# Storing the first image pair by halves and loading less ahead, in a sparse 3x3 convolution

## The chip, the cores and the metric

One core of one Trainium2 chip. The metric is device microseconds of a whole execution; "span" is the part of it that the profile covers, about 1.8 us shorter. Some executions of any kernel are slow as a whole (over 1.5% above the fastest of the same kernel); they are called slow below and are left out of every ratio.

## The reference, cut to what matters

```python
# x: 16 x 64 x 64 x 64 fp32, weight: 128 x 64 x 3 x 3 fp32 with 90% zeros
x_pad = np.pad(x, ((0, 0), (0, 0), (1, 1), (1, 1)))
for b, co, ci, kh, kw in ...:                      # five loops, written out in the original
    output[b, co] += weight[co, ci, kh, kw] * x_pad[b, ci, kh:kh+64, kw:kw+64]
```

An ordinary 3x3 convolution. The input is 16.8 MB, the output 33.6 MB, both fp32 in HBM.

## The kernel before

Two images make a pair: 64 input channels of each fill the 128 partitions. A pair has 4 blocks of 16 rows; I number the blocks of all pairs through as steps, step = 4 x pair + block. For each step but the first, POOL adds neighbouring rows (`s`), PE multiplies, ACT copies one shared product, DVE adds it to the others and writes fp32 rows of `o`, which SP stores. x is loaded by POOL's DMA queue, which casts fp32 to bf16 on the way.

```python
xs = [x_pool.tile([128, H, W], BF16, name=f"x{p}") for p in range(NP)]   # all of x stays on chip
nc.sync.dma_start(out=w_sb, in_=...)                                     # weights, fp32
nc.sync.dma_start(out=x_head[:, 0:HEAD, :], in_=pair(0)[:, 0:HEAD, :])   # "the head": 32 rows, fp32
nc.gpsimd.dma_start(out=xs[0][:, HEAD:H, :], in_=pair(0)[:, HEAD:H, :])
...
EARLY, CUT = 4, 24
for p in range(1, EARLY):
    load(p)                          # whole pairs up front
load(EARLY, 0, CUT)                  # and 24 rows of the next
...
keep_busy(27)                        # matmuls on zeros, to wake PE's clock
...                                  # weights are cast and transposed
keep_busy(28)
...
for p in range(NP):
    ...
    last = p == NP - 1
    for blk in range(4):
        ...
            twos(p, o, r0)
            if p == 1 and blk == 3:
                load(EARLY, CUT, H)
            elif p > 1 and blk == 3 and p + EARLY - 1 < NP:
                load(p + EARLY - 1)
        ...
        if last and blk % 2 == 1:    # last pair: stored by halves
            ...
    if not last:                     # others: stored whole, after the fourth block
        for n in range(2):
            nc.sync.dma_start(out=out[2 * p + n], in_=o[n])
```

Of the kernel before, what the change touches and what calls it, by code (L numbers as in the profile page):

```python
# [8 lines left out]
FP32 = mybir.dt.float32  # L9
BF16 = mybir.dt.bfloat16  # L10
# [17 lines left out]
def kernel(  # L28
# [6 lines left out]
    nc = tc.nc  # L35

    B, C_IN, H, W = x.shape
    C_OUT, _, KH, KW = weight.shape
    assert (B, C_IN, H, W) == (16, 64, 64, 64) and (C_OUT, KH, KW) == (128, 3, 3)
    NP = B // 2  # L40
    HEAD = 32

    const_pool = ctx.enter_context(tc.tile_pool(name="const", bufs=1))
# [4 lines left out]
    psum_pool = ctx.enter_context(  # L48
        tc.tile_pool(name="psum", bufs=8, space=bass.MemoryType.PSUM)
    )  # L50
# [4 lines left out]
    def pair(p):  # L55
        return x[2 * p : 2 * p + 2].rearrange("n i h w -> (n i) h w")
# [10 lines left out]
    def load(p, a=0, b=H):  # L67
        nc.gpsimd.dma_start(out=xs[p][:, a:b, :], in_=pair(p)[:, a:b, :])  # L68



    EARLY, CUT = 4, 24
    for p in range(1, EARLY):
        load(p)
    load(EARLY, 0, CUT)


    idle_rhs = const_pool.tile([128, 128], BF16, name="idle_rhs")
    nc.vector.memset(idle_rhs, 0.0)  # L79
    idle_ps = psum_pool.tile([128, 128], FP32, name="ps")  # L80

    def keep_busy(n):
        for _ in range(n):
            nc.tensor.matmul(idle_ps, idle_rhs, idle_rhs, start=True, stop=True)  # L84

    keep_busy(27)



# [8 lines left out]
    def cast_x(copy, a, b):  # L98
        copy(out=xs[0][:, a:b, :], in_=x_head[:, a:b, :])  # L99
# [24 lines left out]
    nc.vector.tensor_copy(out=wT[:, G0], in_=ps0)  # L124
    ps2 = transposed(G2)
    nc.scalar.copy(out=wT[:, G2], in_=ps2)
    keep_busy(28)
    cast_x(nc.scalar.copy, 9, 18)
    difference(G01, ps0)
    difference(G21, ps2)  # L130
# [26 lines left out]
    def direct(p, o, r0, rows):  # L157
        ps = product(
            [(xs[p], G1, r0, 1), (xs[p], G0, r0 - 1, 1), (xs[p], G2, r0 + 1, 1)], rows
        )  # L160
        nc.scalar.copy(out=o[0][:, r0 : r0 + rows, :], in_=ps[0])  # L161
        nc.vector.tensor_copy(out=o[1][:, r0 : r0 + rows, :], in_=ps[1])  # L162

    def twos(p, o, r0):
        t0 = r0 // 2
        s = s_pool.tile([128, 8, W], BF16, name="s")
        nc.gpsimd.tensor_tensor(  # L167
            out=s, in0=xs[p][:, r0 : r0 + 16 : 2, :], in1=xs[p][:, r0 + 1 : r0 + 16 : 2, :], op=ADD
        )
        shared = product([(s, G1, 0, 1)], 8)  # L170
        pc = []
        for n in range(2):
            c = p_pool.tile([128, 8, W], FP32, name="pc")
            nc.scalar.copy(out=c, in_=shared[n])  # L174
            pc.append(c)
        even = [(xs[p], G21, r0 + 1, 2), (xs[p], G0, r0 - 1, 2)]
        odd = [(xs[p], G01, r0, 2), (xs[p], G2, r0 + 2, 2)]
        for first, terms in ((r0, even), (r0 + 1, odd)):
            ps = product(terms, 8)
            for n in range(2):  # L180
                nc.vector.tensor_tensor(  # L181
                    out=o[n][:, first : r0 + 16 : 2, :], in0=ps[n], in1=pc[n], op=ADD
                )

    for p in range(NP):
        o = [o_pool.tile([C_OUT, H, W], FP32, name="o") for _ in range(2)]
        last = p == NP - 1
        for blk in range(4):
            r0 = 16 * blk
            if BLOCKS[p][blk] == "T":  # L190
                twos(p, o, r0)


                if p == 1 and blk == 3:
                    load(EARLY, CUT, H)
                elif p > 1 and blk == 3 and p + EARLY - 1 < NP:
                    load(p + EARLY - 1)
            else:
                for r, rows in ((r0, 8), (r0 + 8, 8)):
                    direct(p, o, r, rows)  # L200
            if last and blk % 2 == 1:
                for n in range(2):
                    rows = slice(r0 - 16, r0 + 16)
                    nc.sync.dma_start(out=out[2 * p + n][:, rows, :], in_=o[n][:, rows, :])
        if not last:
            for n in range(2):
                nc.sync.dma_start(out=out[2 * p + n], in_=o[n])

# [29 lines left out]
```

## Time and profile before

| | before |
|---|---|
| time, median of 4 runs beside the changed kernel | 126.5 us (126.4 to 126.55) |
| span of the profiled run | 124.7 us |
| first convolution matmul | 7.35 us |
| loads queued up front | 9.47 MB of HBM reads |
| first store issued | 21.83 us |
| HBM traffic | 50.62 MB |

The lines that carry this stand in the prediction below. To read them: a slice is 1/40 of the span, "DMA" is the share of time in which the 16 DMA engines have a packet open, and "GB/s" counts a casting load by the bf16 bytes that it writes, which is half of what it reads. So where I compare DMA work I use the load queue (q0) twice and the store queue (q1) once.

### The profile page before, as it was taken

The page shows a single profiled execution, that of the slowest core. Times are in us where ns is not written, and L with a number is a line of the kernel's source. Part 1 is how long each engine was busy: PE and PEld are TensorE (multiplying, and loading weights), DVE is VectorE, ACT ScalarE, POOL GpSimd, SP SyncE. Part 2 cuts the span into 40 slices and gives each one's busy share as a digit, 9 for nine tenths or more (in the row PEclk, how much of TensorE's full clock was granted, in tenths as well). Part 3 has the DMA queues.
Part 4 walks back from the last instruction along what each step waited for, and adds up shares of the span by engine and source line. Part 5 has one row for each costly group of instructions (what it writes and reads, how often), then busy time and mean ns, then how long its engine had stood idle before and what let it go on. Part 6 is the DMA issues. An engine that isn't in the chain of part 4 may idle for free.

```text
span 124.7 us, 2543 instructions
## 1 busy us (share of the span) xinstructions
PE 109.0 (87%) x1030; PEld 59.5 (48%) x1030; DVE 82.3 (66%) x135; ACT 39.0 (31%) x71; POOL 41.1 (33%) x46
## 2 busy tenths in 40 slices
PE   6999999999999999999999999999999999940000
PEld 6755555555555555555555555555555555510000
DVE  0354777877787778777877787778777878870000
ACT  4545323333333333333333333333333333300000
POOL 6427343533353335333533333333333300000000
PEclk9999999999999999999999999999999999998555
DMA  4999999999999999999999999999999999999991
GB/s 127 356 225 213 215 218 213 211 400 311 350 409 410 318 297 344 436 310 323 302 433 310 318 315 423 420 449 420 426 431 420 436 426 441 415 412 420 428 381 53
DMA packets 4188, 42.93 MB, mean 344 GB/s; under 512 B 464, under 2 KB 464, under 8 KB 976
## 3 DMA queue, kind: packets, MB, share of 16 engines
q1 hardware_dynamic: 2880, 34.90, 66.6%
q0 software_dynamic: 1296, 7.86, 30.8%
q8 instruction: 8, 0.13, 0.4%
q14 instruction: 4, 0.03, 0.1%
HBM read 17.07 MB, written 33.55 MB: 406 GB/s over the span
## 4 chain that ended last, share of the span: by engine, by line
PE 82%; DMA 5%; DVE 1%; issue 1%; DVEq 0%; SPq 0%
PE ps L148 82%; DMA o<-in_x_dram 5%; DVE o L181 1%; DVEq L233 0%; DVE x L99 0%; SPq L60 0%; DVEq L181 0%
## 5 line engine op out<-in xcount | busy, mean ns | idle before, releaser
L181 DVE TENSOR_TENSOR o<-ps,pc 128x512 f32<-128x512 f32 x124 | 77.8, 686 | 22.1 <-PE ps L148 19.8
L148 PE MATMUL ps<-x,wT 64*128 64x504 bf16 (+3 forms) x780 | 88.7, 373 | 0.3 <-DVE x L99 0.3
L148 PEld LDWEIGHTS <-wT 64*128 64x128 bf16 x966 | 54.4, 94 | 48.9 <-issue 0.3
L167 POOL TENSOR_TENSOR s<-x 128x512 bf16<-128x512 bf16 x31 | 35.6, 1151 | 57.5 <-PE ps L148 43.2
L174 ACT COPY pc<-ps 128x512 f32<-128x512 f32 x62 | 33.3, 589 | 64.0 <-issue 61.8
L148 PE MATMUL ps<-s,wT 64*128 64x512 bf16 (+1 forms) x186 | 25.7, 377 | 0.0
L84 PE MATMUL ps<-idle_rhs 128*128 128x128 bf16 x55 | 4.8, 265 | 1.0 <-DVE idle_rhs L79 1.0
L84 PEld LDWEIGHTS <-idle_rhs 128*128 128x128 bf16 x55 | 4.4, 123 | 1.0 <-DVE idle_rhs L79 1.0
L68 POOL DMA_DIRECT2D x<-in_x_dram x8 | 4.4, 561 | 0.0
L103 DVE CAST w_bf<-w_sb 128x192 bf16<-128x192 f32 (+1 forms) x4 | 1.1, 346 | 2.9 <-DMA w_sb<-in_weight_dram 2.9
L162 DVE COPY o<-ps 128x512 f32<-128x512 f32 x2 | 1.4, 692 | 2.0 <-PE ps L148 2.0
L161 ACT COPY o<-ps 128x512 f32<-128x512 f32 x2 | 1.2, 586 | 2.4 <-PE ps L148 2.4
L99 ACT CAST x<-o 128x576 bf16<-128x576 f32 (+1 forms) x2 | 1.5, 804 | 0.8 <-DMA o<-in_x_dram 0.8
L99 DVE CAST x<-o 128x576 bf16<-128x576 f32 x1 | 0.5, 460 | 1.9 <-DMA o<-in_x_dram 1.9
L103 ACT ACT_TABLE_LOAD x1 | 1.3, 1283 | 0.7 <-PEq L222 0.7
L109 PE MATMUL ps<-ident,w_bf 128*128 128x128 bf16 x9 | 1.1, 296 | 0.3 <-DVE w_bf L103 0.3
L103 ACT CAST w_bf<-w_sb 128x64 bf16<-128x64 f32 (+1 forms) x2 | 0.7, 416 | 1.8 <-DMA w_sb<-in_weight_dram 1.8
L109 PEld LDWEIGHTS <-w_bf 128*128 128x128 bf16 x9 | 0.8, 128 | 0.7 <-DVE w_bf L103 0.7
L113 DVE TENSOR_TENSOR wT<-ps,wT 128x384 bf16<-128x384 f32 x2 | 1.0, 548 | 0.0
L63 POOL DMA_DIRECT2D x<-in_x_dram x1 | 0.7, 693 | 0.8 <-POOLq L222 0.8
L79 DVE MEMSET idle_rhs<- 128x64 uint32 x1 | 0.1, 112 | 0.8 <-PEq L222 0.8
L122 ACT CAST wT<-ps 128x384 bf16<-128x384 f32 x1 | 0.5, 480 | 0.4 <-PE ps L109 0.4
(8 smaller groups left out, 2.0 us busy)
## 6 DMA issues: line engine op xcount, KB each, us to landing
out_dram<-o SPq DMA_DIRECT2D x14, 2048.0 KB, 17.4
x<-in_x_dram POOLq DMA_DIRECT2D x6, 1024.0 KB, 15.8
out_dram<-o SPq DMA_DIRECT2D x4, 1024.0 KB, 11.4
o<-in_x_dram SPq DMA_DIRECT2D x1, 1024.0 KB, 5.6
x<-in_x_dram POOLq DMA_DIRECT2D x1, 640.0 KB, 14.0
x<-in_x_dram POOLq DMA_DIRECT2D x1, 512.0 KB, 7.5
x<-in_x_dram POOLq DMA_DIRECT2D x1, 384.0 KB, 24.6
w_sb<-in_weight_dram SPq DMA_DIRECT2D x1, 288.0 KB, 3.0
```

The lines of the kernel that those rows point to most:

```text
L68: nc.gpsimd.dma_start(out=xs[p][:, a:b, :], in_=pair(p)[:, a:b, :])
L84: nc.tensor.matmul(idle_ps, idle_rhs, idle_rhs, start=True, stop=True)
L99: copy(out=xs[0][:, a:b, :], in_=x_head[:, a:b, :])
L103: copy(out=w_bf4[:, g, a:b, :], in_=w_v[:, k : k + b - a, :])
L109: nc.tensor.matmul(wps[:, j, :], src, ident, start=True, stop=True)
L113: nc.vector.tensor_tensor(out=wT[:, g], in0=wps, in1=wT[:, G1], op=SUB)
L148: nc.tensor.matmul(ps[n][:, lo:hi, c_lo:c_hi], tap(g, kw, n), src[q, a:b:step, c_lo + kw - 1 : c_hi + kw - 1], start=(i == 0), stop=(i == ...
L161: nc.scalar.copy(out=o[0][:, r0 : r0 + rows, :], in_=ps[0])
L162: nc.vector.tensor_copy(out=o[1][:, r0 : r0 + rows, :], in_=ps[1])
L167: nc.gpsimd.tensor_tensor(out=s, in0=xs[p][:, r0 : r0 + 16 : 2, :], in1=xs[p][:, r0 + 1 : r0 + 16 : 2, :], op=ADD)
L174: nc.scalar.copy(out=c, in_=shared[n])
L181: nc.vector.tensor_tensor(out=o[n][:, first : r0 + 16 : 2, :], in0=ps[n], in1=pc[n], op=ADD)
```

## The change

Its intent is to let the first stores start at 16 us and not at 22, by putting fewer loads ahead of them, and to make up for that with loads issued later. The 55 narrow matmuls on zeros become 14 wide ones.

```diff
-    EARLY, CUT = 4, 24
+    EARLY, CUT = 2, 56
     for p in range(1, EARLY):
         load(p)
     load(EARLY, 0, CUT)
+    later = {5: [(2, CUT), (3,)], 7: [(4,)], 11: [(5,)], 15: [(6,)], 19: [(7,)]}
-    idle_rhs = const_pool.tile([128, 128], BF16, name="idle_rhs")
+    idle_rhs = const_pool.tile([128, 512], BF16, name="idle_rhs")
 ...
-            nc.tensor.matmul(idle_ps, idle_rhs, idle_rhs, start=True, stop=True)
-    keep_busy(27)
+            nc.tensor.matmul(idle_ps, idle_rhs[:, 0:128], idle_rhs, start=True, stop=True)
+    keep_busy(7)
 ...
-    keep_busy(28)
+    keep_busy(7)
 ...
+    HALVES = (0, NP - 1)
 ...
-                if p == 1 and blk == 3:
-                    load(EARLY, CUT, H)
-                elif p > 1 and blk == 3 and p + EARLY - 1 < NP:
-                    load(p + EARLY - 1)
+                for args in later.get(4 * p + blk, ()):
+                    load(*args)
 ...
-            if last and blk % 2 == 1:
+            if p in HALVES and blk % 2 == 1:
 ...
-        if not last:
+        if p not in HALVES:
```

I call the loads issued after step 5 (8 rows of pair 2, then pair 3) "the reload".

More of the change, by code (lines that the diff above doesn't have):

```diff
@@ L75 @@
     load(EARLY, 0, CUT)
-    idle_rhs = const_pool.tile([128, 128], BF16, name="idle_rhs")
+    later = {5: [(2, CUT), (3,)], 7: [(4,)], 11: [(5,)], 15: [(6,)], 19: [(7,)]}
+    idle_rhs = const_pool.tile([128, 512], BF16, name="idle_rhs")
     nc.vector.memset(idle_rhs, 0.0)
-    idle_ps = psum_pool.tile([128, 128], FP32, name="ps")
+    idle_ps = psum_pool.tile([128, 512], FP32, name="ps")
     def keep_busy(n):
         for _ in range(n):
-            nc.tensor.matmul(idle_ps, idle_rhs, idle_rhs, start=True, stop=True)
-    keep_busy(27)
+            nc.tensor.matmul(idle_ps, idle_rhs[:, 0:128], idle_rhs, start=True, stop=True)
+    keep_busy(7)
     w_v = w_sb.rearrange("o (i k) -> o k i", k=KH * KW)
@@ L183, in twos @@
                 )
+    HALVES = (0, NP - 1)
     for p in range(NP):
         o = [o_pool.tile([C_OUT, H, W], FP32, name="o") for _ in range(2)]
-        last = p == NP - 1
         for blk in range(4):
```

## The prediction

> **What bounds the kernel now.** I read the page's head and its slices first, to see which resource never rests.
>
> ```profile
> span 124.7 us, 2543 instructions
> PE 109.0 (87%) x1030; PEld 59.5 (48%) x1030; DVE 82.3 (66%) x135; ACT 39.0 (31%) x71; POOL 41.1 (33%) x46
> ...
> DMA  4999999999999999999999999999999999999991
> GB/s 127 356 225 213 215 218 213 211 400 311 350 409 410 318 297 344 436 310 323 302 433 310 318 315 423 420 449 420 426 431 420 436 426 441 415 412 420 428 381 53
> DMA packets 4188, 42.93 MB, mean 344 GB/s; under 512 B 464, under 2 KB 464, under 8 KB 976
> ...
> q1 hardware_dynamic: 2880, 34.90, 66.6%
> q0 software_dynamic: 1296, 7.86, 30.8%
> ...
> HBM read 17.07 MB, written 33.55 MB: 406 GB/s over the span
> ```
>
> Each slice is 3.12 us. The DMA row is full from the second slice to the last but one, while PE has gone idle four slices before the end. The GB/s row seems to say that the first half runs at half rate. It does not: the loads cast fp32 to bf16 and are counted by what they write (42.93 MB moved, against 17.07 + 33.55 = 50.62 MB at HBM; the gap of 7.69 MB is about the 7.86 MB of the load queue q0). So 213 GB/s of pure loading is 426 GB/s read, the rate of pure storing.
>
> The bound on time is therefore 50.62 MB / 0.427 MB per us = 118.5 us, 0.427 being my middle of the store-only rows below. Then I asked by windows where the other 6 us of the span lie.
>
> ```profile
> 2.00:4.00 2.00, 2.00 (x20) 1.79 (x17) 0.20 (x1) 0.22 (x2) 1.93 (x5) 1.00 1.01 339
> ...
> 22.00:24.00 2.00, 2.00 (x24) 1.05 (x20) 1.40 (x3) 0.76 (x2) 1.46 (x2) 1.00 0.99 172
> 24.00:26.00 2.00, 2.00 (x22) 1.07 (x20) 1.45 (x3) 1.07 (x2) 1.05 (x1) 1.00 1.10 334
> ...
> 90.00:100.00 10.00, 10.00 (x98) 5.30 (x96) 7.76 (x13) 3.22 (x6) 3.58 (x4) 1.00 1.02 433
> 100.00:110.00 10.00, 10.00 (x96) 5.23 (x94) 7.82 (x13) 3.22 (x6) 0.00 (x0) 1.00 0.99 423
> ...
> 121.00:122.00 1.00, 0.00 (x0) 0.00 (x0) 0.00 (x0) 0.00 (x0) 0.00 (x0) 0.50 0.58 246
> 122.00:123.00 1.00, 0.00 (x0) 0.00 (x0) 0.00 (x0) 0.00 (x0) 0.00 (x0) 0.50 0.20 82
> 123.00:124.00 1.00, 0.00 (x0) 0.00 (x0) 0.00 (x0) 0.00 (x0) 0.00 (x0) 0.50 0.00 0
> ```
>
> The last three columns are granted clock, DMA share, GB/s. Lost are 1.8 us ahead of the first packet, about 2.8 us after 121 in which engines finish unevenly and the program closes, a dip at 22 to 24 where loads hand over to stores (172 where 213 is usual: 2 us x 41/213 = 0.4 us), and the rest in a slow first few us. There is no idle stretch of DMA to recover in the middle.
>
> The second candidate is PE. The chain of waits names it, and needs care.
>
> ```profile
> PE 82%; DMA 5%; DVE 1%; issue 1%; DVEq 0%; SPq 0%
> ...
> 7.35 102.09 PE ps L148 x954
> ```
>
> PE runs without a gap from 7.35 to 109.44, and the last DVE addition ends at 111.98. But that chain ends there, and the span goes on for 12.7 us of storing. The last two half stores, 2.10 MB, need 2.10 / 0.427 = 4.9 us plus about 2 us to land: a store queue with no backlog would have been done near 119. Hence the end is set by DMA with some 5 us of backlog in front of it, and PE has that slack at the end only.
>
> **What the Trainium skill says.** "DMA: Bandwidth & Descriptors", section "Where 436 GB/s comes from": the fabric ceiling is 435.2 GB/s for a core. The trace agrees: 423 to 433 in store-only windows, so at most 2 or 3% is left in the rate. The same page, "Issuing engines are not separate DMA queues": transfers started by different engines share the same 16 DMA engines and interleave. So a store started earlier takes its bandwidth from a load; the mixed slices agree (310 to 320 GB/s counted, where loads count half). The same page, "Anatomy of one DMA — SWDGE (gpsimd) path": about 2.0 us fixed plus bytes / 436 GB/s, mostly the receipt at the end. The trace's 288 KB weight load, though on the other path, lands in 3.0 us against an estimate of 2.7 from that. "TensorE: Matmul & The Clock Gate", section "Wait — 56ns, not 53.3ns?": 106.7 and 426.7 ns for 128 and 512 columns cold, 55.6 and 215.7 warm. The trace has 27 narrow ones in 3.06 us (113 each) and 28 in 1.73 us (62 each).
>
> **The change, part by part.**
>
> (a) Zeros on PE. 55 x 128 = 7,040 columns become 14 x 512 = 7,168. First batch: 7 x 427 = 2.99 us for 3.06; second: 7 x 216 = 1.51 for 1.73 (estimates from the page named). The memset is four times as wide, perhaps 0.2 us later. The first convolution matmul waits for the cast of the input head, which waits for its load (landing at 6.8), so 7.35 stays. 41 matmuls and weight loads vanish, worth nothing on the path.
>
> (b) Loads up front. A pair is 2.10 MB read. Before: weights 0.29 + four pairs 8.39 + 24/64 of one 0.79 = 9.47 MB, drained at 1.8 + 9.47/0.427 = 24.0 us, where the windows show stores taking over. After: 0.29 + 2 x 2.10 + 56/64 x 2.10 = 6.32 MB, drained at 16.6, or near 17.3 with the slow start.
>
> (c) Stores of pair 0.
>
> ```profile
> 13.37 2.51 DVE L181 TENSOR_TENSOR o<-ps,pc 128x512 f32<-128x512 f32 x4 [1.30 <-PE ps L148]
> ...
> 15.70 1.16 POOL L167 TENSOR_TENSOR s<-x 128x512 bf16<-128x512 bf16 x1
> ...
> 21.83 14.22 SPq L207 DMA_DIRECT2D out_dram<-o  x4
> ```
>
> Block 1 is done for image 0 one addition before 15.88, so its half can be issued near 15.3 and that of image 1 near 16.0, instead of both at 21.8. The second halves go out at the old time. They reach DMA just as the loads run dry at about 17.
>
> (d) Loads moved. The rest of pair 2 and pair 3 follow the sum of step 5, which ends at 16.86: issued at 16.9 and 17.4. The remaining pairs keep their places, after steps 7 (22.9), 11, 15 and 19. By 23 us both programs have asked for the same bytes: pairs up to 4 and the stores of pair 0, 0.29 + 10.49 + 4.19 = 14.97 MB, good until 1.8 + 14.97/0.427 = 36.9 us. The next stores are issued at 34.57 in the trace, about 2 us before that. From there on the two programs are the same.
>
> Sum on the path: bytes 0; rate about +0.1 (pair 0 goes in 8 KB rows); the old dip of 0.4 us is replaced by one at about 17, of the same kind but closer to empty, 0.3 to 1.0 us, and perhaps a smaller one where loads come back near 21. Net: 0 to +0.7 us; I take +0.2, and so 126.7 us.
>
> **The rivals.**
>
> Earlier stores bring the end forward. The intent of the change, and true if DMA had idle time in the first 22 us or if the last stores were late for want of an earlier start. The full DMA row speaks against both: each store byte moved to 17 displaces a load byte to later, one for one. The most it could give is the dip (0.4) and a luckier tail: 125.7.
>
> DMA starves near 17. Stores are released by DVE, loads by POOL, both behind PE. Should the first half come out 1 us later, or a fresh queue need 2 to 3 us to get under way (at 22 the first stores seem to flow only after 24), DMA lies partly idle between 17 and 19, and nothing makes that up, as the rest is full: 127.5 to 128.5. For it: only 1.3 to 2 us between issue and dry queue. Against: SP is waiting for DVE alone, so it issues at once.
>
> ```profile
> SPq L207 <- DVE o L181: 90.1, 14, 20.1
> ```
>
> Pair 3 comes late and stalls PE. Issued at 17.4, it shares DMA with the stores: 2.36 MB at half of 427 is 11 us, plus start and receipt, so it lands at 29 to 33. POOL first needs it at its step 12, which starts at 37.76 in the trace. A margin of about 5 us or more; and a stall of 1 or 2 us of PE would only eat slack at the end. I give it little.
>
> PE stays cold. If 7 wide matmuls fail to wake the clock, the first 16 convolution matmuls or so cost twice, about 1.7 us, and the first half is late by that: this feeds the second rival. The work per us is as dense as before, so unlikely.
>
> **Range and chances.** Mechanism: one resource, never idle, the same bytes in another order. So 126.7 us, with 125.7 to 127.8 for 8 in 10: down by the dip and the tail, up by a starved 1 us and a second dip. The 2% limits are 124.0 and 129.0. Faster needs 2.5 us, more than all the recoverable loss in the middle: 3%. Slower needs both starving and a cold clock: 4%. Within 2%: 93%.
>
> **What would show it.** Right: a DMA row full from slice 2 on; GB/s rising over 300 near 17 instead of 24, and the pure-store stretch at over 420 starting at the same 78 us as before; PE still gapless from about 7.35, its last matmul near 109.4; stores landing until about 123. Step (c): SP's first store issue near 15.3. Step (d): POOL's two loads at about 17. Wrong: a DMA share well under 1 near 17 to 19 or 36 (starving), PE waiting on anything after 7.4 (late load), or store windows above 435 GB/s, or a last packet ahead of 121 us, which would mean that the order of reads and writes does change the rate, which I say it does not.

## The result, and the profile after

The changed kernel took 128.3 us in the median of 4 runs (127.78 to 128.81), the kernel before 126.5 us. The ratio is 1.0143, 95% interval 1.0101 to 1.0184. Ratios here are the mean time of one kernel's fast runs over that of the other's of the same rounds, so not quite the ratio of the medians. It is slower by 1.4%, within the 2% that counts as the same, but outside the range that I gave, and its own runs lie a whole microsecond apart.

The head of the page of the changed kernel, as shown of before:

```profile
span 126.0 us, 2467 instructions
...
PE   6989999999999999999999999999999999930000
...
DMA  4999998999999999999999999999999999999991
GB/s 146 339 225 211 215 300 193 265 278 289 273 322 416 325 309 333 424 296 320 343 424 307 302 333 442 416 439 416 432 421 437 442 421 416 426 426 419 429 395 55
...
HBM read 17.07 MB, written 33.55 MB: 402 GB/s over the span
```

The bytes are the same, 402 GB/s stands where 406 stood, and the DMA row is as good as full again. But look at the GB/s row: the stores do come in at the sixth slice (300, near 16 to 19 us), and the seventh (19 to 22 us) falls to 193. The windows say more exactly where; the last three columns are granted clock, DMA share and GB/s:

```profile
16.00:18.00 2.00, 2.00 (x22) 1.07 (x20) 1.27 (x4) 1.06 (x2) 1.87 (x3) 1.00 0.96 270
18.00:20.00 2.00, 2.00 (x22) 1.08 (x20) 1.87 (x4) 0.73 (x2) 0.95 (x2) 1.00 0.95 364
20.00:22.00 2.00, 2.00 (x24) 1.06 (x21) 1.41 (x3) 0.35 (x1) 0.53 (x1) 1.00 0.87 120
22.00:24.00 2.00, 2.00 (x22) 1.11 (x20) 1.40 (x3) 1.08 (x2) 1.47 (x2) 1.00 1.02 269
```

From 20 to 22 us DMA counts as 87% busy and moves 120 GB/s. Even if all of it were loads counted at half, that would be 240 of the usual 427. A busy share says that packets were open, not that they moved. The queues' own rows tell the bytes (queue, packets, MB, share of the 16 engines' time). The changed kernel from 20 to 23 us:

```profile
q0 software_dynamic: 149, 0.25, 69.9%
q1 hardware_dynamic: 38, 0.24, 19.4%
```

and the kernel before at its own handover, 22 to 25 us:

```profile
q0 software_dynamic: 156, 0.47, 92.1%
q1 hardware_dynamic: 9, 0.15, 11.7%
```

Three microseconds at 427 GB/s are 1.28 MB at HBM. The changed kernel moved 0.24 + 2 x 0.25 = 0.74 MB and lost 1.3 us there; the kernel before moved 0.15 + 2 x 0.47 = 1.09 MB and lost 0.4 us. The difference, about 0.8 us, is most of the 1.3 us between the two spans. About 0.5 us more went just before, where the loads hand over to the stores, from 16 to 20 us:

```profile
q1 hardware_dynamic: 131, 1.02, 64.2%
q0 software_dynamic: 55, 0.24, 29.7%
```

That is 1.02 + 2 x 0.24 = 1.50 of 1.71 MB. The kernel before moved 2 x 1.28 MB from 16 to 22 us and lost nothing there.

Was there nothing to do? The timeline of the changed kernel says there was:

```profile
14.12 2.51 DVE L183 TENSOR_TENSOR o<-ps,pc 128x512 f32<-128x512 f32 x4 [1.30 <-PE ps L150]
...
16.12 7.32 SPq L206 DMA_DIRECT2D out_dram<-o  x4
...
17.22 1.10 POOL L68 DMA_DIRECT2D x<-in_x_dram  x2
```

The first half store was issued at 16.12 and the second one could be when DVE's fourth addition had ended, at 16.63 (SP waits for DVE alone); the reload was issued at 17.22 and about 17.8. The instruction that issues the second half store is long in this run:

```profile
16.65 2.30 SPq L206 DMA_DIRECT2D out_dram<-o  x1
```

In the kernel before, the 14 instructions of this kind took 0.35 us in the median and 1.35 us at most. Those requests are 2.10 + 2.36 MB, over 10 us of DMA work, all issued by 19.0 us. Yet in DMA's records the reload's first packet, of its 8-row piece, starts at 19.84, and the second image's half only at 20.98, when the first image's half is all but through. So DMA was not short of requests at 20 us. What it had open then was mostly the 8-row piece, in packets of 1 KB; the second half store and the large piece of the reload were issued but still to come.

The start was late too. The chain of waits of the changed kernel:

```profile
1.18 6.38 DMA o<-in_x_dram
...
8.09 102.09 PE ps L150 x954
```

In this run the head of the input landed at 7.55 us and not at 6.81, so PE began 0.74 us later, and the first stores with it. PE then ran as before, 102.09 us without a gap. This delay is not a second sum to add: the bytes that DMA failed to move account for the longer span by themselves (see the sum over all profiles).

### The profile page after: what moved, and what is told of

Read it like the earlier page. It is cut to its first block, busy times and chain, and to the rows that moved or that the text cites. A ratio compares the mean times of both kernels' runs of the same rounds, so it can differ in the third digit from the quotient of the medians.

```text
span 126.0 us, 2467 instructions
## 1 busy us (share of the span) xinstructions
PE 109.6 (87%) x989; PEld 57.5 (46%) x989; DVE 82.4 (65%) x135; ACT 39.0 (31%) x71; POOL 41.1 (33%) x46
## 4 chain that ended last, share of the span: by engine, by line
PE 81%; DMA 5%; DVE 1%; issue 1%; DVEq 0%; SPq 0%
PE ps L150 81%; DMA o<-in_x_dram 5%; DVE o L183 1%; DVEq L235 0%; DVE x L101 0%; SPq L60 0%; DVEq L183 0%
## 5 line engine op out<-in xcount | busy, mean ns | idle before, releaser
L183 DVE TENSOR_TENSOR o<-ps,pc 128x512 f32<-128x512 f32 x124 | 77.8, 685 | 22.1 <-PE ps L150 19.8
L86 PE MATMUL ps<-idle_rhs 128*128 128x512 bf16 x14 | 5.6, 568 | 1.2 <-DVE idle_rhs L81 1.2
L86 PEld LDWEIGHTS <-idle_rhs 128*128 128x128 bf16 x14 | 1.8, 137 | 3.7 <-issue 2.4
## 6 DMA issues: line engine op xcount, KB each, us to landing
out_dram<-o SPq DMA_DIRECT2D x12, 2048.0 KB, 17.8
```

The costliest lines, as they stand in the source:

```text
L86: nc.tensor.matmul(idle_ps, idle_rhs[:, 0:128], idle_rhs, start=True, stop=True)
L183: nc.vector.tensor_tensor(out=o[n][:, first : r0 + 16 : 2, :], in0=ps[n], in1=pc[n], op=ADD)
```

## The experiments

Fifteen runs, each on one chip beside its own runs of the kernel before. Of those, one (201.5 us) and two (131.36 and 128.66) were slow and are left out. Times of single runs are given where they differ; the profile shows one run of each.

I call "the hole" the stretch after the up-front loads in which DMA moves little. Theory: the time lost is DMA's, between 16 and 24 us, and it comes from the margin between the up-front loads running dry and the stores and reload reaching the engines. Rivals: the wide zeros delay the start; half stores or small pieces cost rate by themselves.

### Each part alone

**wide_only**: the kernel before with only the zeros changed.

```diff
-    EARLY, CUT = 2, 56
+    EARLY, CUT = 4, 24
-    later = {5: [(2, CUT), (3,)], 7: [(4,)], ...
+    later = {7: [(4, CUT)], ...
-    HALVES = (0, NP - 1)
+    HALVES = (NP - 1,)
```

(The diffs of this group are against the changed kernel.)

> The kernel before with the 14 wide zero matmuls alone; loads and stores as before. Hole theory (the loss is DMA left short of work at 20 to 22 us): 126.3 to 126.7 us, as before, and DMA full throughout. Rival, late start (the 0.74 us by which the first convolution matmul came later is due to the wide zeros and carries to the end): first convolution matmul near 8.1 us instead of 7.35 and 127.0 to 127.4 us.

Measured: 126.43 us beside 126.64, ratio 1.0005 (0.9962 to 1.0048). The late start was there: the second batch of zeros,

```profile
5.25 2.62 PE L86 MATMUL ps<-idle_rhs 128*128 128x512 bf16 x7
```

took longer than the 1.73 us of the narrow one, with 374 ns for each matmul, between the 427 and 216 ns of the prediction's estimate, and the first convolution matmul came at 7.79 us. With four pairs of loads queued this cost nothing: the hole theory holds here, and the rival falls for the loads of before.

**halves_only**: the loads and zeros of before, the first pair by halves.

```diff
-    EARLY, CUT = 2, 56      (and later, and the zeros)
+    EARLY, CUT = 4, 24      (as in the kernel before)
```

> The kernel before with the stores of the first pair in halves alone; loads as before, narrow zeros. Hole theory: loads still queue until 24 us, so nothing runs dry: 126.2 to 126.8 us, with stores mixed in from about 17 us. Rival (8 KB rows or the earlier mixing of stores with loads cost rate by themselves): 127.2 us or more with DMA full and a lower GB/s count in 16 to 24 us.

Measured: 126.85 us beside 126.64, just over the range that the theory gave, ratio 1.0024 (0.9998 to 1.0050). No dry spell (from 17 to 20 us it moved 0.14 + 2 x 0.49 = 1.12 of 1.28 MB), and no gain either, which fits the prediction's argument that a store moved forward displaces a load one for one.

**loads_only**: the shorter up-front loading and the reload, the first pair stored whole.

```diff
-    HALVES = (0, NP - 1)
+    HALVES = (NP - 1,)      (and the narrow zeros)
```

> The kernel before with the shorter up-front loading and the later reloading alone; the first pair stored whole at 22 us, narrow zeros. Hole theory: after the up-front loads end near 17.3 us there is nothing until the reloads' first packets near 20 to 21.7 us: about 3 us of DMA lost, 128.5 to 130 us, worse than the changed kernel. Rival (loads in smaller pieces are harmless, it is the half stores that hurt): 126.3 to 127 us.

Measured: 129.00 us, ratio 1.0172 (1.0136 to 1.0209; one of its four runs was slow at 130.53 and is left out). As the theory said. The half stores are the cure for the shorter loading, and an incomplete one.

**all_but_wide**: the changed kernel with narrow zeros.

```diff
-    idle_rhs = const_pool.tile([128, 512], BF16, ...      keep_busy(7) ... keep_busy(7)
+    idle_rhs = const_pool.tile([128, 128], BF16, ...      keep_busy(27) ... keep_busy(28)
```

> The changed kernel with the narrow zeros of before. Hole theory: the same as the changed kernel, 127.8 to 128.6 us, with the hole at 20 to 22 us. Rival, late start by wide zeros: first convolution matmul back at 7.35 us and 127.0 to 127.5 us.

Measured: 127.18 us (127.11 to 127.24, and one run of 128.47), ratio 1.0078 (1.0020 to 1.0136). Three of the four runs fell in the rival's range and one in the theory's, and the first convolution matmul was back at 7.35 us in the profiled run. That spoke for the rival; with two kinds of runs it did not decide about the zeros, and narrow_again below took it up.

### Moving the reload, the pieces and the zeros

**changed_again**: the changed kernel, unedited.

> The changed kernel once more, on the chip of the next three. Hole theory plus a late start by the wide zeros: 1.2 to 1.9 us over the kernel before of the same rounds; second batch of zeros 2.4 to 2.6 us long, first convolution matmul at 7.8 us or later, DMA short of work for about 2 us between 20 and 23 us. Rival (the kernel without the wide zeros differed from this one by chip or chance): 0.7 to 1.0 us over before.

Measured: 126.93, 126.97, 128.36 and 128.82 us; ratio 1.0095 (1.0012 to 1.0179). By the ratio that is 1.2 us over the kernel before, the low end of the theory's range, but in two kinds of runs of one kernel on one chip. The profile fell on a good run (126.97), with PE starting at 7.27 us and the second batch of zeros only 1.67 us long, which is not what I had expected.

**reload_at_3**: the reload two steps earlier.

```diff
-    later = {5: [(2, CUT), (3,)], 7: ...
+    later = {3: [(2, CUT), (3,)], 7: ...
```

> The changed kernel with the first reload (8 rows of pair 2, and pair 3) issued after the sum of step 3, near 12.5 us, not after that of step 5, near 17 us. Hole theory: the loads reach DMA before the first ones have drained, nothing runs dry, and the time is within 0.4 us of the kernel before, like the half stores alone. Rival (not the moment of the reload but the small pieces and 8 KB rows cost): no better than the changed kernel of this call.

Measured: 126.64 us beside 126.53, ratio 1.0019 (0.9978 to 1.0061). This one edit takes the loss away, with half stores, 8 KB rows, small pieces and wide zeros all kept. (Its interval and that of changed_again overlap; the pair with the late start below, reload_at_3_late and changed_late, is clearly apart.) It does not beat the kernel before either; none of the fifteen does. Its queues from 12 to 32 us (each GB/s figure is 0.5 us):

```profile
GB/s 180 182 201 229 201 215 215 215 248 201 29 121 320 178 182 410 147 442 131 410 180 360 262 262 311 213 344 426 410 426 442 344 246 279 295 213 295 295 213 377
...
q0 software_dynamic: 549, 2.92, 73.6%
q1 hardware_dynamic: 320, 2.37, 28.8%
```

There is still a dip at 17 to 18 us (29, 121). It is not a handover between the queues, as no store packet starts before 19.4 us: it lies between the last of the up-front loads and the first packets of the 8-row piece. From 19.5 us the two queues take turns every half microsecond (410 and 442 are stores, 147 and 131 loads counted at half).

**one_piece**: no 8-row piece.

```diff
-    EARLY, CUT = 2, 56
+    EARLY, CUT = 2, 64
-    later = {5: [(2, CUT), (3,)], 7: ...
+    later = {5: [(3,)], 7: ...
```

> The changed kernel with 64 rows of pair 2 up front instead of 56, so no 8-row piece: pair 3 is issued 0.55 us earlier and the up-front loads last 0.6 us longer. Hole theory: the hole shrinks by about 1 us, and the time comes to 0.4 to 1.0 us over before. Rival (the lost time is the handing over from stores back to loads, which takes its 1 to 2 us whenever it falls): the same as the changed kernel within 0.3 us.

Measured: 126.51, 126.53, 127.23 and 127.58 us; ratio 1.0032 (0.9980 to 1.0083). In the direction of the theory and about of its size, but the intervals of this kernel and the changed one overlap.

**wide_fewer**: 4 wide zeros in the second batch.

```diff
-    keep_busy(7)
+    keep_busy(4)
```

> The changed kernel with 4 instead of 7 wide zero matmuls in the second batch. If the wide zeros delay the first convolution matmul, and this delay widens the hole: the batch ends before 7 us, the first convolution matmul is back near 7.35 us when the input's head lands by 6.8, and the time is 0.6 to 1.0 us over before. Rival (the zeros are beside the point): the same as the changed kernel of this call within 0.2 us.

Measured: 126.84, 126.89, 127.75 and 127.84 us; ratio 1.0050 (0.9993 to 1.0106). The first convolution matmul was at 7.38 us in the profiled run, and the mean is about as far over the kernel before as the first expectation said and not as the rival did, though the interval overlaps with that of changed_again. But two kinds of runs remained. So the late start by the wide zeros is not what makes the two kinds.

### Moving the start

**before_late** and **changed_late**: more zeros ahead of the first convolution matmul.

```diff
-    keep_busy(28)        (kernel before)
+    keep_busy(52)
-    keep_busy(7)         (changed kernel, second batch)
+    keep_busy(14)
```

> The kernel before with 24 more narrow zero matmuls ahead of the first convolution matmul, which should then come near 8.6 us instead of 7.35. Hole theory: loads queue until 24 us, so a start 1.3 us later is hidden: within 0.3 us of the kernel before. Rival (a late start costs its length whatever the loads): 127.5 us or more.

Measured: 126.71, 127.38 and 128.54 us, and a slow run of 130.39; ratio of the fast ones 1.0084 (0.9991 to 1.0176). The expectation of 0.3 us was missed in two of three. The profiled run, 128.54, had an accident: the head of the input landed at 10.1 us, and PE began at 10.68. The up-front loads ran dry near 25, and the first store's packets came at 26.01. That is the same hole, in the kernel before, once its margin of about 2 us is used up. How much of a 1.3 us delay alone it hides, this run does not show.

> The changed kernel with 7 more wide zero matmuls, first convolution matmul at 8.6 to 9.1 us in every run. Hole theory, with the changed kernel's two kinds of runs (near 126.9 and near 128.5) being early and late starts: all runs near 128.5 us or above, 1.8 to 2.5 us over before, and the first store's packets with nothing queued beside them. Rival (the two kinds are the queues' own affair): two kinds again, one near 127.

Measured: 128.07 to 128.92 us, all four; ratio 1.0149 (1.0099 to 1.0198). PE began at 9.21 us, and no run was of the good kind.

**reload_at_3_late**: the same edit for a delay, with the earlier reload.

```diff
-    later = {5: ...          keep_busy(7)  (second batch)
+    later = {3: ...          keep_busy(14)
```

> The same late start with the reload issued after step 3, whose sum waits for no matmul. Hole theory: the loads are queued until about 22 us, so the late start is hidden as in the kernel before: within 0.5 us of it. Rival: as the changed kernel with the late start.

Measured: 126.67, 126.77 and 127.05 us (and a slow run of 132.31); ratio 1.0027 (1.0002 to 1.0052). PE began at 8.09 us in its profiled run, not at 9.21, but that is just as late as in the changed kernel's first profile, with 0.80 us lost in the sum below and not 2.11. A late start is hidden again when the loads are long enough.

**changed_early**: an attempt at an earlier start.

```diff
-    nc.sync.dma_start(out=x_head[:, 0:HEAD, :], in_=pair(0)[:, 0:HEAD, :])
+    for a, b in ((0, 18), (18, HEAD)):
+        nc.sync.dma_start(out=x_head[:, a:b, :], in_=pair(0)[:, a:b, :])
-    keep_busy(7)         (second batch)
+    keep_busy(2)
```

> The changed kernel with the input's head loaded in two pieces (18 and 14 rows) and only 2 wide zeros in the second batch, so that the first convolution matmul can come near 6 us. Hole theory: stores and reload are issued about 1.3 us earlier, both before the loads run dry at 17 us: within 0.4 us of the kernel before and one kind of run. Rival: 126.9 to 128.5 us in two kinds, as the changed kernel.

Measured: 130.95, 131.07 and 132.07 us (and a slow run of 132.96); ratio 1.0385 (1.0323 to 1.0448). It failed as an early start: PE began at 6.46 us, but the second piece of the head came behind the loads and landed near 11.2, PE stood, and the first store was issued at 19.36. So it became the largest dose of lateness. Its windows:

```profile
18.00:19.00 1.00, 1.00 (x12) 0.52 (x10) 1.00 (x3) 0.00 (x0) 0.00 (x0) 1.00 0.15 31
19.00:20.00 1.00, 1.00 (x12) 0.56 (x10) 0.87 (x2) 0.77 (x2) 0.63 (x1) 1.00 0.00 0
```

Here DMA is plainly empty for more than a microsecond.

### What was still open: the zeros, and the margin from the other side

**changed_third** (unedited), **narrow_again** (as all_but_wide) and **more_up_front**, five rounds each:

```diff
-    EARLY, CUT = 2, 56
+    EARLY, CUT = 3, 24
-    later = {5: [(2, CUT), (3,)], 7: ...
+    later = {5: [(3, CUT)], 7: ...
```

> The changed kernel a third time, beside the next two. Both theories: 0.5 to 2.3 us over the kernel before, single runs spread over 1.5 us or more.

Measured: 128.36 us (127.63 to 128.97), ratio 1.0136 (1.0109 to 1.0164). The profiled run began PE at 7.43 us, early, and still had its hole, 19.5 to 21.5 us. So a late start is not needed for the hole; that it makes it surer and larger is what changed_late and changed_early suggest. That is a part of my theory which falls.

> The changed kernel with the narrow zeros. If the wide zeros add to the loss by a later start: 0.5 us or more below the changed kernel of this call, most runs near 127.1 us. If they are beside the point: the two means within 0.3 us.

Measured: 127.76 us (126.94 to 128.43), ratio 1.0101 (1.0071 to 1.0130). The means of the times are 0.6 us apart, those of the spans are not: 125.93 with wide zeros, 125.95 with narrow ones. The extra time of the wide kernel's runs lies outside the span (1.74 to 3.07 us there, against 1.73 to 1.89 in narrow_again), and what it is the profile cannot say; the runs of the changed kernel beside the result above did not have it (1.75 to 1.91 us). By the times the first expectation was met, by the spans the second. Inside the span the zeros are beside the point.

> The changed kernel with three pairs and 24 rows up front instead of two pairs and 56 rows (1.05 MB, 2.5 us of DMA more), and the other 40 rows reloaded after step 5; half stores and wide zeros kept. Margin theory: the loads run dry near 20 us, after the stores and about when the reload arrives, so it is within 0.5 us of the kernel before, with runs close together. Rival (the loss comes with going over from loads to stores and back, wherever it falls): as the changed kernel of this call.

Measured: 127.20 us, five runs within 127.16 and 127.34; ratio 1.0061 (1.0049 to 1.0073). Half right. The spread is gone, as the margin theory said, but 0.77 us are left where it allowed 0.5. The queued loads did not help against a handover: from 18 to 20 us, with loads still queued and stores already issued at 15.43, DMA moved 0.06 MB of stores and 2 x 0.20 of loads, 0.46 of 0.85 MB. So time can be lost at the handover with loads queued and stores issued, and unequally: 0.4 us in the kernel before, 0.9 us here in those two microseconds.

One rival was left untested: rows of a small piece. In each of these stretches the loads in the engines were mostly those of a piece of few rows, in packets of 3 KB in the kernel before (118 of 165 packets) and more_up_front (61 of 80), and of 1 KB in the changed kernel (119 of 187). Small pieces alone are not enough, as reload_at_3 has the same 8-row piece and one_piece, which has none, still lost 1.08 us in the sum below. But no run changes only the piece, as one_piece also issued pair 3 earlier.

### The sum over all profiles

If the theory is right in its main point, that the loss is DMA's and lies here, then the span of any of these kernels must be a constant plus what DMA failed to move. I take q1 + 2 x q0 from 12 to 32 us against 20 us x 0.427 = 8.54 MB. The rows for the kernel before:

```profile
q0 software_dynamic: 540, 3.02, 75.3%
q1 hardware_dynamic: 151, 2.24, 26.7%
```

which is 2.24 + 6.04 = 8.28 MB, 0.26 short, 0.61 us. For the changed kernel, as first profiled:

```profile
q0 software_dynamic: 505, 2.56, 66.9%
q1 hardware_dynamic: 339, 2.52, 31.3%
```

7.64 MB, 2.11 us. And changed_late:

```profile
q0 software_dynamic: 473, 2.31, 59.5%
q1 hardware_dynamic: 373, 2.79, 36.7%
```

7.41 MB, 2.65 us. In the same way for each profiled run:

| kernel | q1 + 2 x q0, MB | lost, us | span, us | span - lost |
|---|---|---|---|---|
| wide_only | 8.37 | 0.40 | 124.6 | 124.2 |
| before | 8.28 | 0.61 | 124.7 | 124.1 |
| reload_at_3 | 8.21 | 0.77 | 124.8 | 124.0 |
| reload_at_3_late | 8.20 | 0.80 | 125.0 | 124.2 |
| changed_again | 8.09 | 1.05 | 125.1 | 124.0 |
| halves_only | 8.08 | 1.08 | 125.1 | 124.0 |
| one_piece | 8.08 | 1.08 | 125.5 | 124.4 |
| all_but_wide | 8.01 | 1.24 | 125.3 | 124.1 |
| wide_fewer | 7.98 | 1.31 | 126.0 | 124.7 |
| more_up_front | 7.93 | 1.43 | 125.4 | 124.0 |
| changed_third | 7.82 | 1.69 | 125.9 | 124.2 |
| changed kernel | 7.64 | 2.11 | 126.0 | 123.9 |
| before_late | 7.64 | 2.11 | 126.8 | 124.7 |
| narrow_again | 7.62 | 2.15 | 126.7 | 124.5 |
| changed_late | 7.41 | 2.65 | 126.7 | 124.1 |
| loads_only | 7.28 | 2.95 | 127.2 | 124.2 |
| changed_early | 6.73 | 4.24 | 129.2 | 125.0 |

The loss goes from 0.4 to 4.2 us, and the remainder stays at 123.9 to 124.7 but for changed_early, whose start differs too. So it is settled where the time went: in DMA, between 12 and 32 us. Of what made the loss in each, one thing can be read directly: how long a request took from the start of the issuing instruction to its first packet.

| the request | DMA then | issue to first packet |
|---|---|---|
| half store, changed_early | empty | 19.36 to 20.21: 0.8 us |
| half store, changed kernel | loads just ending | 16.12 to 17.18: 1.1 us |
| reload, loads_only | empty | 17.06 to 18.33: 1.3 us |
| store, before | loads running | 21.83 to 24.76: 2.9 us |
| half store, halves_only | loads running | 15.31 to 19.48: 4.2 us |
| half store, more_up_front | loads running | 15.43 to 19.66: 4.2 us |
| reload, changed kernel | stores running | 17.22 to 19.84: 2.6 us |
| reload, narrow_again | stores running | 17.41 to 22.43: 5.0 us |

The Trainium skill, "DMA: Bandwidth & Descriptors", section "Latency and other measured facts", gives about 0.6 us to the first byte for a store from SP and about 1 us for a load from POOL. With DMA empty the runs show a little more than that, 0.8 and 1.3. Behind a running stream of the other queue they show 2.6 to 5.0. The same page, "Queues, rings and completion order", says that each engine takes turns between queues packet by packet; once both queues flow, the turns of 0.5 us above agree, but the first turn comes late. Why, no run here isolates: whether the engines have fetched several rows of the other stream ahead was not tested. Nor is it settled why some handovers lose 0.4 us and others over 1 us with the same requests, which is the difference between changed_again and changed_third. One thing that differs is when the second half store arrives: in changed_again its packets follow those of the first half at once, at 19.91 us; in changed_third and in the changed kernel as first profiled they come at 21.11 and 20.98, and the instruction that issues it took 1.35, 1.89 and 2.30 us. Why that instruction is long is open as well, and narrow_again lost 2.15 us, most of it later, with 1.03.

## Why the prediction was wrong, point by point

- **The bound.** Right. Bytes, PE's 102.09 us and the rates outside the handovers stayed, the end is set by DMA, and the order of reads and writes does not change the steady rate. The argument that earlier stores gain nothing was borne out as well (halves_only).
- **(a) The zeros.** The second batch was estimated at 1.51 us, fully warm, and took 1.67 to 2.62 us at 7 matmuls. "7.35 stays" was wrong for wide_only (7.79). It did not matter for the span. The delay of 8.09 in the profiled run was the head's landing, which varies by itself: it was as late in narrow_again, which has the narrow zeros.
- **(b) When the up-front loads run dry.** 16.6 to 17.3 us predicted; load packets dwindle from 17.0 us. Right.
- **(c) The stores "reach DMA just as the loads run dry at about 17".** Right for the first image's half, issued at 16.12 for a predicted 15.3, with packets from 17.18. Wrong for the second image's, whose packets came at 20.98 in the profiled run, for a predicted issue near 16.0.
- **(d) and the sum: here it failed.** I priced the handover at 17 at 0.3 to 1.0 us and wrote of "perhaps a smaller one where loads come back near 21". The first price held: from 16 to 20 us about 0.5 us was lost. The failed step is the second: it was the larger one, and where loads come back, at 20 to 23 us, 1.3 us was lost. I had taken a request as work at the engines once it was issued and about a microsecond had passed, although the store of the kernel before, issued at 21.83 and seen only after 24, was in front of me; I charged that delay to the stores alone, not to the reload. What the runs showed in its place: the reload issued at 17.2 arrives from 19.8 us on, its small piece first, and the second half store, issued from 16.65 on, at 21.0, when the first half is already through. By these figures the sum on the path is 0.5 + 1.3 - 0.4 = 1.4 us, about the 1.3 us between the spans. Issuing the reload two steps earlier took the loss away (1.0019 for 1.0095 of the changed kernel beside it, and 1.0027 for 1.0149 with the late start). Why the requests take so long stays open.
- **The rivals.** "DMA starves near 17 ... 127.5 to 128.5" named the right size, but for a place where only about 0.5 us was lost, and was given too little weight. Its counter-argument, that SP "issues at once", held for the first half store only: the instruction for the second took 2.30 us. "Pair 3 comes late and stalls PE" did not happen: PE never stood in the changed kernel.
- **The range.** It reached almost as far down as up, for a change that replaces a queue with a dip of 0.4 us by one that depends on arrivals within about 2 us. None of the fifteen runs gained by it, and those of the changed kernel spread over 2 us; the range should have reached 129.

## What to carry to other kernels

Where DMA is the bound, as here, expect no gain from moving transfers about: in fifteen runs it gained nothing and in some it lost. What helped was to issue a queue's next request several microseconds before the other stream ends, not when it ends (reload_at_3); that it is no guarantee, more_up_front shows. Measure that lead from issue to first packet in the trace, and judge a stretch by its bytes, not by its busy share. A schedule that works only with arrivals in time should be tried with a start that comes a microsecond late before it is believed.

## What the Trainium skill lacked or had wrong

- "DMA: Bandwidth & Descriptors", section "Latency and other measured facts": the first-byte times were about met with the engines empty only (0.8 us for a store, 1.3 us for a casting load, from the start of the issuing instruction). Behind a running stream of the other queue it was 2.6 to 5.0 us; the page has no such figure.
- The same page, "Queues, rings and completion order", has nothing on what can be lost where one queue takes over from another: 0.4 us of DMA time in the kernel before, 0.9 us in more_up_front and 1.3 us in the changed kernel, with requests outstanding.
- No page has a measured case of DMA's busy share standing high while little moves: here it was 0.87 at 120 GB/s, in the changed kernel from 20 to 22 us.
